# Stick-breaking attention: the second scan of a unit is issued one step later, behind the copy of the first head's transposed weights, and the copies on VectorE are always the first head's

## The chip, the cores and the metric

The kernel runs on one core of one Trainium2 chip. The metric is the device time of one execution in microseconds (us), and less is better. Engines are named as in the profile: PE is TensorE (PEld its weight loads), DVE VectorE, ACT ScalarE, POOL GpSimd, SP the engine that issues most DMAs.

## What is computed

The model has two layers on 2048 tokens of width 1024. The first layer mixes three kinds of attention: stick-breaking (6 heads of 64), differential (6 heads) and attention to a memory. The change touches only stick-breaking attention, which the reference writes, for each block of 128 queries, as

```
z = einsum('bqhd,bkhd->bhqk', qi, k) * scale
log_1mb = where(strict, log_sigmoid(-z), 0.0)
rc = flip(cumsum(flip(log_1mb, -1), -1), -1)
after = rc - log_1mb
w = where(strict, exp(log_sigmoid(z) + after), 0.0)
out = einsum('bhqk,bkhd->bqhd', w, v)
```

So a weight is the sigmoid of its own score times the product of sigmoid(-z) over all later keys: a running product from the last key to the first.

## The kernel before

The program has these stages: projections of layer 1, stick-breaking, differential attention (with part of the output projection mixed in), the join, and layer 2. Each engine works through its own queue in the order of the program; the queues meet at semaphores.

In stick-breaking (L543 to L650) heads go in pairs: p counts three pairs, t four chunks of 512 queries (from the last to the first), qi four blocks of 128 queries in a chunk, and c the chunks of 512 keys, from the diagonal back to the first. A **unit** (p, t, qi, c) is one block of queries against one chunk of keys for both heads of the pair, 120 units in all, 84 of them 512 keys wide and the others, on the diagonal, 384, 256 or 128. A unit passes four functions:

- `scores(u)`: TensorE writes the scores of both heads into a PSUM tile `psz` (2 buffers).
- `weights(u)`: ScalarE takes two sigmoids of it, `s` (of -z) and `wb` (of z), both heads in one instruction each. Then for each head VectorE runs a scan over `s` (a running product, written into `row`; 0 is added from the PSUM tile `pszero`), and GpSimd multiplies `wb` by `row` (L608).
- `turn(u)`: for each head TensorE transposes the 128-wide blocks of `wb` into a PSUM tile `pstp` (2 buffers), and the tile is copied to SBUF as `wT`. `tblocks` (L472) does both. The copy's engine comes from a pattern that is used letter by letter, A for ScalarE and V for VectorE: with "AAV" over the calls the units repeat in threes: both copies on ScalarE; first head on VectorE and second on ScalarE; first on ScalarE and second on VectorE.
- `values(u)`: TensorE multiplies `wT` with the values into `pspv`. Two units' products are issued together, after every second turn.

The loop over units k issues scores(k+3), turn(k), weights(k+3), and every second time the products of units k-2 and k-1. TensorE, VectorE, ScalarE and the DMAs keep exactly this order (they are pinned, and all their rows carry line L57); GpSimd's is left to the scheduler. At the start of a chunk, `begin` issues the DMAs for the next: for the chunk (2, 1) these are also the loads that differential attention and the first output products need (`kc`, `kd`, `qa`, `mp`, and `rx`, which are weights of the output projection). The scheduler also decides which of the two `pstp` buffers a tile gets, and with that which copy it has to wait for.

Of the kernel before, what the change touches and what calls it, by code (L numbers as in the profile page):

```python
# [17 lines left out]
P = 128  # L18
# [21 lines left out]
SB_AHEAD = 3  # L40
# [26 lines left out]
class Net:  # L67
# [475 lines left out]
    def stick_breaking(self):  # L543

        nc = self.nc
        self.nc = PinnedCore(nc, self.tc, ("sync", "tensor", "vector", "scalar"))
        chunks = [(p, t) for p in range(3) for t in range(NT - 1, -1, -1)]
        units = [(p, t, qi, c) for p, t in chunks for qi in range(3, -1, -1) for c in range(t, -1, -1)]  # L550
        kv, qs, sls, prs, zs, ws, wTs, pvs = {0: self.sb_first[:2]}, {(0, NT - 1): self.sb_first[2]}, {}, {}, {}, {}, {}, {}

        def begin(p, t):
            sls[p, t] = self.load_silu(self.silu[p], t)
            k = chunks.index((p, t)) + 1
            if k < len(chunks):
                qs[chunks[k]] = self.load_qstack(self.sbq[chunks[k][0]], chunks[k][1])
            if t == NT - 2 and p < 2:
                kv[p + 1] = self.load_sb(p + 1)
            if p == 2 and t == FT:  # L560
                self.fill = self.filler()
                steps.extend(next(self.fill))
                for f in steps[:4]:
                    f()
                del steps[:4]
                self.dk, self.dq = {}, {}
                self.load_dq(0, 0, 0)
                for c in range(NT):
                    self.load_dk(0, c)

        def bounds(u):
            p, t, qi, c = u
            n = (4 * t + qi + 1) * P
            return n, c * 512, min(n, c * 512 + 512)

        def scores(u):
            p, t, qi, c = u
            n, lo, hi = bounds(u)
            m, diag, s0 = hi - lo, hi == n, int(lo == 0)
            if qi == 3 and c == t:  # L580
                begin(p, t)
            if c == t:
                prs[p, t, qi] = [self.t("row", F32, [P, 2048]) for _ in range(2)]
                for hh in range(2):
                    nc.gpsimd.memset(prs[p, t, qi][hh][:, n - 1:n], 1.0)
            z = self.psum("z", [P, 2, 512])
            for hh in range(2):
                for k in range(2):
                    self.nc.tensor.matmul(z[:, hh, :m], qs[p, t][:, hh, k, qi * P:(qi + 1) * P], kv[p][0][hh][:, lo:hi], start=(k == 0),
                                          stop=(k == 1 and not diag))  # L590
                if diag:
                    self.nc.tensor.matmul(z[:, hh, m - P:m], self.identb, self.mask[:, 2 * P + 1:3 * P + 1], start=False, stop=True)
            zs[u] = z

        def weights(u):
            p, t, qi, c = u
            n, lo, hi = bounds(u)
            m, s0, z = hi - lo, int(lo == 0), zs.pop(u)
            rest = self.t("s", F32, [P, 2, 512])
            self.nc.scalar.activation(rest[:, :, :m], z[:, :, :m], AF.Sigmoid, scale=-0.125)  # L600
            w = ws[u] = self.t("wb", F32, [P, 2, 512])
            self.nc.scalar.activation(w[:, :, :m], z[:, :, :m], AF.Sigmoid, scale=0.125)
            for hh in range(2):
                prr = prs[p, t, qi][hh]
                self.nc.vector.tensor_tensor_scan(
                    prr[:, lo + s0 - 1:hi - 1][:, ::-1], rest[:, hh, s0:m][:, ::-1], zero.to_broadcast([P, m - s0]),
                    prr[:, hi - 1:hi], ALU.mult, ALU.add)
                nc.gpsimd.tensor_mul(w[:, hh, :m], w[:, hh, :m], prr[:, lo:hi])  # L608

        def turn(u):  # L610
            n, lo, hi = bounds(u)
            w = ws.pop(u)
            wTs[u] = [self.tblocks([w[:, hh, j:j + P] for j in range(0, hi - lo, P)], "AAV") for hh in range(2)]

        def values(u):
            p, t, qi, c = u
            n, lo, hi = bounds(u)
            if qi == 3 and c == t:
                pvs[p, t] = self.psum("pv")
            pv, wT, nj = pvs[p, t], wTs.pop(u), (hi - lo) // P  # L620
            for j in range(nj):
                for hh in range(2):
                    self.nc.tensor.matmul(pv[64 * hh:64 * hh + 64, qi * P:(qi + 1) * P], kv[p][1][:, 4 * c + j, 64 * hh:64 * hh + 64],
                                          wT[hh][:, j * P:(j + 1) * P], start=(hi == n and j == 0), stop=(c == 0 and j == nj - 1))
            if qi == 0 and c == 0:
                mt = self.t("c2")
                self.nc.vector.tensor_mul(mt, pvs.pop((p, t)), sls.pop((p, t)))
                self.dma(self.m1[p, :, t * TC:(t + 1) * TC], mt, nc.scalar if p == 2 and t == 0 else None)

        done, steps = 0, []  # L630
        zero = self.psum("zero")[:, :1]
        nc.vector.memset(zero, 0.0)
        for u in units[:SB_AHEAD]:
            scores(u)
            weights(u)
        for k, u in enumerate(units):
            if k + SB_AHEAD < len(units):
                scores(units[k + SB_AHEAD])
            turn(u)
            if k + SB_AHEAD < len(units):  # L640
                weights(units[k + SB_AHEAD])
            if u[0] == 2 and k > len(units) - 11:
                for f in steps[:1]:
                    f()
                del steps[:1]
            while k - done >= SB_GROUP or k == len(units) - 1 and done <= k:
                for v in units[done:done + SB_GROUP]:
                    values(v)
                done += SB_GROUP
        self.nc = nc  # L650
# [872 lines left out]
```

## Time and profile before

| what | value |
|---|---|
| median of 3 runs | 2544.74 us (2543.16 to 2546.1) |
| profiled execution, its own time | 2546.16 us |
| its span, first to last instruction | 2544.4 us |
| granted TensorE clock, mean over the span | 0.984 |
| stick-breaking, first scan to last transpose copy | about 722 to 1076 us |

The span is what the trace covers; the rest of an execution's own time, 1.8 us here, lies around it. All times in rows are counted from the start of the span. Busy shares are means over stages with different limits, so what follows is read from the stick-breaking stage alone.

### The profile page before, as it was taken

Reading aid. Unit: us, or ns where it says so; the run is one execution under the profiler, and the core shown is the slowest. Engines: PE = TensorE matmul, PEld = TensorE weight load, DVE = VectorE, ACT = ScalarE, POOL = GpSimd, SP = SyncE. Lnnn points to the kernel's source line nnn. Section 1 sums busy time; section 2 is a strip of 40 time slices with the busy share of each in tenths; the row PEclk is TensorE's granted clock in tenths of the full one; section 3 lists DMA queues with packets and bytes.
Section 4 is the critical chain, followed back from the end, with each engine's and each line's share of the span. In section 5 each row is a group of like instructions: output and inputs, shape, how many; then the busy total and the mean of one; then the engine's idle time right before and its main releaser. Section 6 shows DMA issues by size and latency. Waiting matters only on the chain. (4 is left out here: it accounts for less than half of the span.)

```text
span 2544.4 us, 42300 instructions
## 1 busy us (share of the span) xinstructions
PE 2392.6 (94%) x15564; PEld 1939.8 (76%) x15564; DVE 1573.6 (62%) x3657; ACT 1254.2 (49%) x2453; POOL 939.3 (37%) x800
## 2 busy tenths in 40 slices
PE   9999999999999999789889888899999999999998
PEld 7778998888877777557667666778788777777887
DVE  5733222431168888699899899684312676777455
ACT  4443222221158777567677677443212777776100
POOL 0401002750057878611111021464612655534333
PEclk9999999999999999899999999999999999999999
DMA  7643222331334431944543341563323655533641
GB/s 280 208 156 131 82 84 79 127 132 56 107 90 111 93 84 34 215 122 109 128 112 94 103 109 46 181 204 109 86 98 112 163 153 154 144 97 101 199 144 64
DMA packets 199247, 311.60 MB, mean 122 GB/s; under 512 B 17920, under 2 KB 97280, under 8 KB 198528
## 3 DMA queue, kind: packets, MB, share of 16 engines
q1 hardware_dynamic: 198464, 307.83, 40.8%
q8 instruction: 124, 2.03, 0.4%
q10 hardware_dynamic: 576, 1.05, 0.1%
q14 instruction: 83, 0.68, 0.1%
HBM read 204.74 MB, written 104.07 MB: 121 GB/s over the span
## 5 line engine op out<-in xcount | busy, mean ns | idle before, releaser
L57 PE MATMUL psmm<-big,w 128*128 128x512 f32 x1680 | 414.9, 395 | 1.3 <-ACT c L325 1.3
L57 PEld LDWEIGHTS psmm<-big,w 128*128 128x128 f32 x1680 | 306.6, 189 | 59.4 <-ACT c L325 1.5
L57 ACT COPY wT<-pstp 128x512 f32<-128x512 f32 (+3 forms) x400 | 203.4, 525 | 188.6 <-PE pstp L57 185.0
L608 POOL TENSOR_TENSOR wb<-wb,row 128x512 f32<-128x512 f32 (+3 forms) x240 | 262.6, 1117 | 72.8 <-DVE row L57 47.5
L57 DVE TENSOR_TENSOR_SCAN row<-s,row,pszero 128x512 f32<-128x512 f32 (+5 forms) x240 | 254.3, 1105 | 51.8 <-ACT s L57 33.4
L254 PE MATMUL psmm<-big,w 128*128 128x512 f32 x1200 | 275.2, 390 | 0.0
L254 PEld LDWEIGHTS psmm<-big,w 128*128 128x128 f32 x1200 | 225.1, 188 | 46.9 <-issue 0.2
L57 PE MATMUL psmm<-big,mp 128*128 128x512 f32 x1056 | 246.6, 394 | 3.4 <-POOL big L1015 3.4
L57 ACT ACTIVATE row<-row,mn 128x2048 f32<-128x2048 f32 (+7 forms) x192 | 229.8, 1202 | 13.9 <-DVE mn L781 10.1
L57 PEld LDWEIGHTS psmm<-big,mp 128*128 128x128 f32 x1056 | 199.7, 190 | 45.3 <-POOL big L1015 3.8
L775 DVE TENSOR_SCALAR_CACHE_REDUCE row<-psz 128x512 f32<-128x512 f32 (+1 forms) x324 | 200.2, 640 | 20.7 <-PE psz L57 19.8
L1234 DVE TENSOR_TENSOR c<-psmm,c 128x512 f32<-128x512 f32 x62 | 42.7, 691 | 240.3 <-ACT c L1233 240.3
L945 POOL TENSOR_TENSOR mp<-mp,mp 128x640 fp32r<-128x640 f32 x32 | 52.0, 1625 | 343.4 <-ACT mp L57 282.7
L57 PE MATMUL pstp<-ident,wb 128*128 128x128 f32 x816 | 118.2, 277 | 35.4 <-DVE wT L57 15.4
L817 DVE SCALAR_TENSOR_TENSOR row<-row,tiny,row 128x128 f32<-128x128 f32 (+7 forms) x144 | 149.4, 1088 | 0.4
L57 PE MATMUL psmm<-wo,mp 128*128 128x512 f32 x480 | 147.7, 420 | 1.4 <-POOL mp L945 0.9
L209 POOL TENSOR_TENSOR w<-w,w 128x1024 fp32r<-128x1024 f32 x20 | 48.8, 2440 | 256.3 <-ACT w L208 107.5
L1233 ACT ACTIVATE c<-psmm 128x512 f32<-128x512 f32 x62 | 36.8, 596 | 212.8 <-PE psmm L254 204.5
L57 PE MATMUL pstp<-ident,row 128*128 128x128 f32 x816 | 130.5, 281 | 6.4 <-ACT wT L57 5.6
L57 PEld LDWEIGHTS pstp<-ident,wb 128*128 128x128 f32 x816 | 92.2, 141 | 56.6 <-POOL wb L608 24.8
L1191 ACT ACTIVATE e<-e,tiny 128x256 f32<-128x256 f32 (+1 forms) x192 | 94.7, 494 | 60.5 <-DVE e L1189 60.1
L57 PEld LDWEIGHTS pstp<-ident,row 128*128 128x128 f32 x816 | 99.6, 143 | 30.8 <-ACT wT L57 13.4
(232 smaller groups left out, 5003.0 us busy)
## 6 DMA issues: line engine op xcount, KB each, us to landing
silu<-c SPq DMA_DIRECT2D x54, 256.0 KB, 2.3
sl<-silu SPq DMA_DIRECT2D x54, 256.0 KB, 3.3
qs<-sbq SPq DMA_DIRECT2D x48, 256.0 KB, 5.3
cs<-rope SPq DMA_DIRECT2D x24, 512.0 KB, 4.6
kc<-k SPq DMA_DIRECT2D x36, 320.0 KB, 5.0
w<-in_we_dram SPq DMA_DIRECT2D x20, 512.0 KB, 3.6
raw<-in_wo_dram SPq DMA_DIRECT2D x20, 512.0 KB, 3.8
rx<-in_x_dram SPq DMA_DIRECT2D x32, 256.0 KB, 2.7
```

What stands on the lines that cost most here:

```text
L57: return self.tc.keep_in_program_order(f(*a, **k))
L209: eng.tensor_sub(lo[:, sl], raw[:, sl], hi[:, sl].bitcast(F32))
L254: self.nc.tensor.matmul(ps, w[a][:, c, :], self.xpart(t, c, b), start=(c == k == 0), stop=(c == 7 and k == 2))
L608: nc.gpsimd.tensor_mul(w[:, hh, :m], w[:, hh, :m], prr[:, lo:hi])
L775: nc.vector.tensor_scalar(e[:, col + lo:col + lo + n0], z[:, :n0], -scale, before, ALU.mult, ALU.min, accum_out=acc)
L817: self.nc.vector.scalar_tensor_tensor(x[:, lo:hi], y[:, lo:hi], cf[hh][:, w:w + 1], x[:, lo:hi], ALU.mult, ALU.add)
L945: self.nc.gpsimd.tensor_sub(ml, m, mh.bitcast(F32))
L1191: nc.scalar.activation(e[:, hh, ns:], e[:, hh, ns:], AF.Exp, bias=nmx[:, hh:hh + 1], scale=-1.0, accum_out=s[:, hh:hh + 1])
L1233: nc.scalar.activation(sg, ps, AF.Sigmoid)
L1234: nc.vector.tensor_mul(sg, ps, sg)
```

## The change

A unit's two scans are now issued apart. `weights(k+3)` still issues both sigmoids and the first head's scan with its product, but the second head's scan and product are put off into a list. The next step's `turn` takes them out after it has issued the first head's transposes and their copy, and before the second head's transposes. So in step k VectorE's queue has: copy of unit k's first head, second scan of unit k+2, first scan of unit k+3. The patterns change too: the first heads' copies go V, V, A, and the second heads' copies are all on ScalarE. As before, two units in three have one copy on VectorE.

```
             w = ws[u] = self.t("wb", F32, [P, 2, 512])
             self.nc.scalar.activation(w[:, :, :m], z[:, :, :m], AF.Sigmoid, scale=0.125)
-            for hh in range(2):
+
+            def scan(hh):
                 prr = prs[p, t, qi][hh]
                 self.nc.vector.tensor_tensor_scan(
                     prr[:, lo + s0 - 1:hi - 1][:, ::-1], rest[:, hh, s0:m][:, ::-1], zero.to_broadcast([P, m - s0]),
                     prr[:, hi - 1:hi], ALU.mult, ALU.add)
                 nc.gpsimd.tensor_mul(w[:, hh, :m], w[:, hh, :m], prr[:, lo:hi])
+            scan(0)
+            second.append(lambda: scan(1))
 
         def turn(u):
             n, lo, hi = bounds(u)
             w = ws.pop(u)
-            wTs[u] = [self.tblocks([w[:, hh, j:j + P] for j in range(0, hi - lo, P)], "AAV") for hh in range(2)]
+            wTs[u] = []
+            for hh in range(2):
+                wTs[u].append(self.tblocks([w[:, hh, j:j + P] for j in range(0, hi - lo, P)], "A" if hh else "VVA"))
+                if second and not hh:
+                    second.pop(0)()
...
         for u in units[:SB_AHEAD]:
             scores(u)
             weights(u)
+            if u != units[SB_AHEAD - 1]:
+                second.pop(0)()
```

The rows below show the program's order at units 58 to 63, in the second pair of heads. A scan stands in them as SCALAR_TENSOR_TENSOR, the numbers are those of the tiles, and a line's two `row` tiles are the first and the second head's.

VectorE before: `s_8076` is unit 61's, `s_8124` unit 62's, `s_8151` unit 63's; `pstp_8062` is the first head of unit 58 and `pstp_8118` the second head of unit 59.

```order
L57 SCALAR_TENSOR_TENSOR row_7978<-s_8049,row_7978,pszero_5912 128x512
L57 SCALAR_TENSOR_TENSOR row_7979<-s_8049,row_7979,pszero_5912 128x512
L57 COPY wT_8067<-pstp_8062 128x512
L57 SCALAR_TENSOR_TENSOR row_7978<-s_8076,row_7978,pszero_5912 128x511
L57 SCALAR_TENSOR_TENSOR row_7979<-s_8076,row_7979,pszero_5912 128x511
L57 COPY wT_8122<-pstp_8118 128x384
L57 SCALAR_TENSOR_TENSOR row_8101<-s_8124,row_8101,pszero_5912 128x256
L57 SCALAR_TENSOR_TENSOR row_8102<-s_8124,row_8102,pszero_5912 128x256
```

VectorE now, from the first scan of unit 60 on (`s_8049`): `pstp_8060` is the first head of unit 58 and `pstp_8135` the first head of unit 60.

```order
L57 SCALAR_TENSOR_TENSOR row_7976<-s_8049,row_7976,pszero_5912 128x512
L57 COPY wT_8065<-pstp_8060 128x512
L57 SCALAR_TENSOR_TENSOR row_7977<-s_8049,row_7977,pszero_5912 128x512
L57 SCALAR_TENSOR_TENSOR row_7976<-s_8076,row_7976,pszero_5912 128x511
L57 SCALAR_TENSOR_TENSOR row_7977<-s_8076,row_7977,pszero_5912 128x511
L57 SCALAR_TENSOR_TENSOR row_8099<-s_8124,row_8099,pszero_5912 128x256
L57 COPY wT_8140<-pstp_8135 128x512
L57 SCALAR_TENSOR_TENSOR row_8100<-s_8124,row_8100,pszero_5912 128x256
```

A copy stood behind both scans of a unit two steps ahead; it now stands behind the first of them alone, and the second scan comes after it. Where the three-unit pattern has no copy on VectorE (unit 59 here) the two scans stand together as before.

ScalarE before, at the turns of units 59 and 60 and the sigmoids of units 62 and 63:

```order
L57 COPY wT_8116<-pstp_8112 128x384
L57 ACTIVATE s_8124<-psz_8105 128x2x256
L57 ACTIVATE wb_8126<-psz_8105 128x2x256
L57 COPY wT_8142<-pstp_8137 128x512
L57 COPY wT_8149<-pstp_8144 128x512
L57 ACTIVATE s_8151<-psz_8132 128x1024
```

ScalarE now, at the same place:

```order
L57 COPY wT_8114<-pstp_8110 128x384
L57 COPY wT_8122<-pstp_8118 128x384
L57 ACTIVATE s_8124<-psz_8103 128x2x256
L57 ACTIVATE wb_8126<-psz_8103 128x2x256
L57 COPY wT_8149<-pstp_8144 128x512
L57 ACTIVATE s_8151<-psz_8130 128x1024
```

Of every three units, one (unit 59) had its sigmoids behind the first head's copy alone. Now the sigmoids of every unit stand behind a copy of a second head's transposes. The number of copies on ScalarE is the same. TensorE's instructions stand in the same order as before through the whole program.

## Rows read from the trace of the kernel before

**Rows 1.** Busy time, share of the span and instructions of each engine, whole span

```profile
PE 2392.6 (94%) x15564; PEld 1939.8 (76%) x15564; DVE 1573.6 (62%) x3657; ACT 1254.2 (49%) x2453; POOL 939.3 (37%) x800
```

**Rows 2.** Busy time in one stretch of stick-breaking: each engine's us (instructions), granted clock, DMA

```profile
core 0: us, PE busy (x) PEld busy (x) DVE busy (x) ACT busy (x) POOL busy (x), PEclk, DMA share, GB/s
740.00:1018.00 278.00, 261.85 (x2510) 213.35 (x2507) 246.76 (x275) 220.48 (x331) 221.57 (x276) 1.00 0.32 75
```

**Rows 3.** Waits in the stretch 740 to 1018: us in total, times, longest us

```profile
ACT wT L57 <- PE pstp L57: 56.8, 63, 2.3
...
DVE row L57 <- ACT s L57: 27.8, 31, 2.2
...
PE pstp L57 <- DVE wT L57: 12.4, 22, 1.5
...
PE pstp L57 <- POOL wb L608: 2.1, 4, 0.8
...
DVE wT L57 <- PE pstp L57: 1.1, 2, 0.7
```

**Rows 4.** Timeline of VectorE, 889 to 899: start us, us, instructions, idle before

```profile
890.26 2.46 DVE L57 TENSOR_TENSOR_SCAN row<-s,row,pszero 128x512 f32<-128x512 f32 x2 [0.71 <-ACT s L57]
892.62 0.67 DVE L57 COPY wT<-pstp 128x512 f32<-128x512 f32 x1
893.21 2.44 DVE L57 TENSOR_TENSOR_SCAN row<-s,row,pszero 128x511 f32<-128x511 f32 x2
895.56 0.54 DVE L57 COPY wT<-pstp 128x384 f32<-128x384 f32 x1
896.01 1.38 DVE L57 TENSOR_TENSOR_SCAN row<-s,row,pszero 128x256 f32<-128x256 f32 x2
898.51 1.28 DVE L57 TENSOR_TENSOR_SCAN row<-s,row,pszero 128x512 f32<-128x512 f32 x1 [1.12 <-ACT s L57]
```

**Rows 5.** Timeline of TensorE, 889 to 899

```profile
893.04 0.92 PE L57 MATMUL pstp<-ident,wb 128*128 128x128 f32 x6
893.71 1.18 PE L57 MATMUL psz<-kd,qs 128*128 128x512 f32 x4
894.73 0.60 PE L57 MATMUL pstp<-ident,wb 128*128 128x128 f32 x4
896.24 0.63 PE L57 MATMUL pstp<-ident,wb 128*128 128x128 f32 x4 [0.92 <-DVE wT L57]
896.80 1.75 PE L57 MATMUL pspv<-wT,kd 128*64 128x128 f32 x28
```

**Rows 6.** Timeline of ScalarE, 889 to 899

```profile
896.96 0.58 ACT L57 COPY wT<-pstp 128x512 f32<-128x512 f32 x1 [1.01 <-PE pstp L57]
897.45 1.03 ACT L57 ACTIVATE s<-psz 128x1024 f32<-128x1024 f32 x1
```

**Rows 7.** Groups of VectorE's instructions, 740 to 1018: xcount | busy us, mean ns | idle before

```profile
L57 DVE TENSOR_TENSOR_SCAN row<-s,row,pszero 128x512 f32<-128x512 f32 x77 | 94.2, 1267 | 18.7 <-ACT s L57 18.4 <-issue 0.2
L57 DVE COPY wT<-pstp 128x512 f32<-128x512 f32 x47 | 31.5, 670 | 0.8 <-PE pstp L57 0.7
```

**Rows 8.** Copies by engine, 740 to 1018: ns min/median/max, first and last start us, forms

```profile
L57 ACT COPY wT<-pstp x132: 265/586/687, 741.7 to 1017.4; 128x512 f32<-128x512 f32 x95, 128x256 f32<-128x256 f32 x14, 128x384 f32<-128x384 f32 x12, 128x128 f32<-128x128 f32 x11
L57 DVE COPY wT<-pstp x67: 264/667/692, 740.8 to 1017.0; 128x512 f32<-128x512 f32 x47, 128x384 f32<-128x384 f32 x7, 128x128 f32<-128x128 f32 x7, 128x256 f32<-128x256 f32 x6
```

**Rows 9.** Timeline of SP's DMA issues, 900 to 1075

```profile
1018.34 3.59 SPq L57 DMA_DIRECT2D qs<-sbq  x4
...
1048.27 8.82 SPq L113 DMA_DIRECT2D kd<-dfk  x8
1057.96 0.35 SPq L57 DMA_DIRECT2D rx<-in_woute_dram  x1
```

**Rows 10.** Waits of SP's DMA queue, 900 to 1080: us in total, times, longest us

```profile
SPq L57 <- PE psz L57: 27.3, 1, 27.3
```

**Rows 11.** Timeline of ScalarE, 1050 to 1135, at the end of stick-breaking

```profile
1067.02 0.62 ACT L57 CAST wo<-rx 128x512 fp32r<-128x512 f32 x1 [15.34 <-DMA rx<-in_woute_dram]
```

**Rows 12.** Timeline of TensorE, 1050 to 1135

```profile
1052.88 1.31 PE L57 MATMUL pspv<-wT,kv 128*64 128x128 f32 x20
1068.27 0.87 PE L57 MATMUL pstp<-ident,wb 128*128 128x128 f32 x3 [14.08 <-ACT wT L57]
```

**Rows 13.** Waits in the whole stage, 718 to 1077

```profile
PE pstp L57 <- DVE wT L57: 15.4, 26, 1.5
```

More of the change, by code (lines that the diff above doesn't have):

```diff
@@ L602, in weights, with scan @@
             self.nc.scalar.activation(w[:, :, :m], z[:, :, :m], AF.Sigmoid, scale=0.125)
-            for hh in range(2):
+            def scan(hh):
                 prr = prs[p, t, qi][hh]
@@ L608, in weights @@
                 nc.gpsimd.tensor_mul(w[:, hh, :m], w[:, hh, :m], prr[:, lo:hi])
+            scan(0)
+            second.append(lambda: scan(1))
         def turn(u):
@@ L612, in turn @@
             w = ws.pop(u)
-            wTs[u] = [self.tblocks([w[:, hh, j:j + P] for j in range(0, hi - lo, P)], "AAV") for hh in range(2)]
+            wTs[u] = []
+            for hh in range(2):
+                wTs[u].append(self.tblocks([w[:, hh, j:j + P] for j in range(0, hi - lo, P)], "A" if hh else "VVA"))
+                if second and not hh:
+                    second.pop(0)()
         def values(u):
@@ L628, in values @@
                 self.dma(self.m1[p, :, t * TC:(t + 1) * TC], mt, nc.scalar if p == 2 and t == 0 else None)
-        done, steps = 0, []
+        done, steps, second = 0, [], []
         zero = self.psum("zero")[:, :1]
@@ L635, in stick_breaking @@
             weights(u)
+            if u != units[SB_AHEAD - 1]:
+                second.pop(0)()
         for k, u in enumerate(units):
```

## Prediction

> **What bounds the kernel now.** I read the page first: TensorE is busy 94% of the span and VectorE 62% [rows 1], but these are means over stages, and the change lives in one. So I read the table of busy times for that stage, from 740, when the pipeline is full, to 1018, where the loads of the next stage begin. There TensorE is busy 261.85 of 278.00 us and VectorE 246.76, ScalarE 220.48, GpSimd 221.57, with the clock at full grant [rows 2]. No engine is full. TensorE has 16.2 us idle, VectorE 31.2.
>
> The list of waits says who holds whom [rows 3]. TensorE's own waits are few: 12.4 us in 22 waits for a VectorE copy out of a `pstp` buffer, 2.1 us in 4 for GpSimd's products. VectorE idles 27.8 us for ScalarE's `s`, and ScalarE 56.8 us for transposes. So it is a ring. The timeline shows one turn of it. The copy of unit 59's second head stands behind both scans of unit 61 and starts at 895.56, when they are through [rows 4]. Its transposes had been done long before: they are among the six at 893.04 [rows 5]. The buffer is free at 896.1, and only then, at 896.24, can TensorE transpose unit 60's second head, after 0.92 us of idling [rows 5]. ScalarE copies that at 896.96 after 1.01 us of idling, takes the next `s` at 897.45 [rows 6], and VectorE's next scan, at 898.51, has waited 1.12 us for it [rows 4]. So one late copy on VectorE costs TensorE, ScalarE and VectorE about 1 us each, one after the other. From the scan at 893.21 to the scan at 898.51 the ring took 5.3 us for two units.
>
> What do the engines need for two full units? Scans follow each other every 1.2 us (two from 893.21 to the next start at 895.56), and a copy of 0.67 has 0.59 to the next start [rows 4, 7]. Two units are four scans and on average 4/3 copies: 4.7 + 0.8 = 5.5 us. The ring is as long as the work, so any unevenness shows as a wait. That is how I read a stage in which nobody is full.
>
> At the stage's end something else binds. TensorE stands still for 14.08 us before 1068.27 [rows 12], because ScalarE waits 15.34 us for a weight load `rx` [rows 11]. That load is issued at 1057.96, behind a train of loads that SP starts at 1018.34 [rows 9], and SP had waited 27.3 us for TensorE's scores before that start, since they free the `qs` buffers [rows 10]. So the train starts when TensorE reaches a certain unit, and ends some 48.7 us later whatever the engines do in between. What is gained before 1018 moves the train and everything behind it; what is gained between 1018 and 1053 only lengthens the 14 us of idling.
>
> **The change, part by part.** No instruction is added or removed; TensorE's order stays, and the two scans, two products and copies of each unit keep their durations.
>
> (a) A VectorE copy moves ahead of one scan, so it starts 1.2 us earlier. The 22 waits of 12.4 us average 0.56, the longest is 1.5 [rows 3]. Moved by 1.2, all but the longest go, and of that one at most 0.3 is left: **-12**. From below the bound is nothing (another wait ends at the same moment), from above TensorE's whole idle time in the stretch, 16.2 [rows 2]. The whole stage has 4 more such waits, 3.0 us [rows 13]; some of them lie behind 1018, where they are covered by the loads, so I count none.
>
> (b) A copy now can be wanted sooner. The first head's tile is often the buffer that the next unit's first transposes need, and where no products stand between, TensorE comes back to it after four transposes and one block of scores: about 0.5 + 1.0 us (894.73 and 896.24 give 0.56 for four transposes up to the products; 893.71 to 894.73 the scores [rows 5]). A copy that starts as its tile is done takes 0.67 [rows 7]; with VectorE up to a scan of 1.2 behind it is done at 1.9, late by up to 0.4. Products stand between at every second step, so about half of the 67 copies [rows 8] are exposed. From 0 to 33 x 0.4 = 13 us. I take 0.06 for each of the 33, **+2**, since VectorE is that far behind only where it has no idle time before a scan, and 31 scans do have it [rows 3].
>
> (c) The second scan comes one copy later, 0.59 us, and so do GpSimd's product and the transposes behind it. TensorE waits for products only 4 times, 2.1 us [rows 3], and the transposes come two units later, some 5.5 us. The cover is this lead of two units: **0**. Without it, 67 x 0.59 = 40 us.
>
> (d) The copies on VectorE are now in front of a scan, so a copy whose transposes aren't done holds a scan. Today the copy waits for them twice, 1.1 us [rows 3], because it stands 1.2 later. If a third of the 67 copies waited half of that, VectorE would lose 22 x 0.6 = 13 us; it has 31.2 idle [rows 2], and the held scan is the one with two units of lead: **0**, at worst 13.
>
> (e) Every unit's sigmoids now follow the second head's copy. In one unit of three (199 copies [rows 8] are about 100 units, so 33 units) they followed the first's, and now come later by four transposes, 0.45 to 0.6 [rows 5]. From 0 to 33 x 0.6 = 20 us on ScalarE's path to VectorE. VectorE has a second scan of the unit before and a copy to do meanwhile, and in the other two units this is already so. I take a twentieth, **+1**.
>
> (f) A few DMA issues and GpSimd instructions change places around the boundary to the next stage: the last stores and loads of `m` before two of `rx`. One issue takes 0.35 us [rows 9]: **0**, within 1 either way.
>
> Sum: -12 + 2 + 1 = -9. The profiled execution took 2546.16, 1.4 above the median of the runs; 2546.16 - 9 = 2537, against the median 2544.74 - 9 = 2535.7. I say **2536**. As a check, the stretch would be 269 us, with TensorE 97% and VectorE 92% busy, which still leaves slack.
>
> **The rivals.**
>
> *VectorE is the bound, and order doesn't help it.* VectorE's work stays 246.76 us, and its idle time stays if ScalarE's `s` comes no sooner: then TensorE's waits for copies turn into waits for products. For it: with 5.5 us of work for two units VectorE has no margin over the ring. Against it: its own idle time in the example comes from its own late copy. Time: no change, 2542 to 2547.
> The Trainium skill bears on this (Perfetto Trace Analysis, Identifying the Most-Contended Engine): it says matmul busy share is no good measure of TensorE and weight-load busy share is to be used, while for VectorE occupancy is fair. By it TensorE stands at 213.35 of 278, 77%, and VectorE at 89% [rows 2] is the engine to relieve, which this change doesn't do; it would give the time of this rival. The rows agree on the order of the two shares, not on its conclusion, since VectorE's idle time begins with a wait that its own copies cause.
>
> *The gain is hidden by the load train.* If the train ended at a fixed time, 2545. Against it: SP's 27.3 us wait for the scores [rows 10] ties its start to TensorE. I put it with the first.
>
> *Slower: the sigmoids behind the second head.* Place: ScalarE at 33 units. Price: up to 0.6 each, 20 us, less the 12 of (a): +8, 2553. It decides against the change from a delay of 0.52 a unit that nothing covers (17 - 12 = +5). For it: 27.8 us of VectorE's idle time end with `s` [rows 3]. Against it: two units in three live with it already, and VectorE's queue holds a scan more at that moment.
>
> *More than I count.* All of TensorE's idle time goes: -16.2 and up to 2 from the stage's opening, 2527.
>
> **How the numbers follow.** Forecast (2531 to 2539.5) 0.51, more than I count 0.11, no change or hidden 0.25, slower 0.13. A difference of 0.2%, 5.1 us, is about what a measurement of this kernel can tell from none. Faster 0.62, same 0.25, slower 0.13. The range, 2527 to 2548, leaves out the slower rival and a tail below; the likeliest case's own range is 2531 to 2539.5.
>
> **What would show it.** (a) right: TensorE's waits for a VectorE copy before 1010 fall from 12.4 to under 4. (b): what is left of them stands before first heads. (d): VectorE's waits for transposes rise from 1.1 to several us, without a longer stage. (e) wrong: VectorE's idle time for `s` rises over 27.8. The stretch from 740 to SP's `qs` issue, now at 1018.34, should end near 1009, with the idle time before the `rx` cast still about 15. If the stage ends sooner and the whole doesn't, the loads hid it; if TensorE's waits go and VectorE's for `s` grow as much, VectorE was the bound.

## The result, and the profile after

| what | before | after |
|---|---|---|
| median of the runs, us | 2544.82 (2543.16 to 2546.1, 4 runs) | 2531.59 (2527.61 to 2532.59, 4 runs) |
| ratio | | 0.9943, 95% interval 0.993 to 0.9956 |
| profiled execution, us | 2546.16 | 2527.61 |

The change made the kernel 13.2 us faster. The forecast was 2536, in a range of 2527 to 2548; the time lies just inside the low end of the likeliest case's own range, 2531 to 2539.5. The profiled execution is the fastest of the four, so its 18.6 us overstate the gain. Of the executions below one, of the kernel with three buffers, took 3348.97 us at a granted clock of 0.651, against 0.973 in the profiled one, and is left out of that kernel's numbers.

TensorE runs the same 15564 matmuls in the same order in both traces, so equal ones can be laid side by side. At the last matmul before stick-breaking the execution after is 1.1 us ahead (718.3 against 719.4), before the change acts. The lead then grows through the stage: 4.0 at 800.6, 8.4 at 868, 11.4 at 933, and 14.7 when SP issues `qs`. So the stage gives 13.6 up to there; the prediction had put that issue near 1009. From there to the end of the program 3.9 more come in small steps, which the median doesn't confirm.

Busy time of each engine from 740 to SP's `qs` issue, now at 1003.66, in the columns of [rows 2]:

```profile
740.00:1003.66 263.66, 257.72 (x2496) 212.50 (x2495) 244.82 (x273) 218.26 (x329) 221.92 (x272) 1.00 0.35 79
```

The stretch took 278.34 us and takes 263.66. TensorE's idle time in it went from 16.2 to 5.9, VectorE's from 31.6 to 18.8, while VectorE's work per unit is the same. (The stretch after starts 1.7 us further on in the program, the lead at 740, so it holds 16 matmuls fewer.) The waits of that stretch, which answer to [rows 3] (us in total, times, longest us), with the weight loads' own:

```profile
ACT wT L57 <- PE pstp L57: 45.1, 53, 2.1
...
DVE row L57 <- ACT s L57: 10.5, 17, 1.6
...
PEld pstp L57 <- POOL wb L609: 6.1, 9, 1.1
...
PE pstp L57 <- DVE wT L57: 3.8, 8, 0.7
DVE wT L57 <- PE pstp L57: 3.5, 8, 0.8
```

VectorE's copies hold TensorE for 3.8 us where it was 12.4, and VectorE idles 10.5 us for ScalarE's `s` where it was 27.8. The row of PEld was not among the rows before the prediction. The kernel before has this one, in the list for the weight loads from 740 to 1018.34:

```profile
PEld pstp L57 <- POOL wb L608: 20.1, 28, 1.2
```

Most waits for GpSimd's products (`wb`) are recorded at the transposes' weight loads: 20.1 us in 28 before, 6.1 in 9 after. The rows of PE showed 4 of them, 2.1 us, and show none now. The two lists can't be added: before, 12.4 of TensorE's 16.2 us of idle time end with VectorE's copies, so most of the 20.1 lies beside matmuls that were still running.

VectorE's timeline after, which answers to [rows 4]:

```profile
881.39 1.28 DVE L57 TENSOR_TENSOR_SCAN row<-s,row,pszero 128x512 f32<-128x512 f32 x1 [0.16 <-ACT s L57]
882.59 0.67 DVE L57 COPY wT<-pstp 128x512 f32<-128x512 f32 x1
883.17 4.25 DVE L57 TENSOR_TENSOR_SCAN row<-s,row,pszero 128x512 f32<-128x512 f32 x4
887.33 0.67 DVE L57 COPY wT<-pstp 128x512 f32<-128x512 f32 x1
887.92 1.91 DVE L57 TENSOR_TENSOR_SCAN row<-s,row,pszero 128x256 f32<-128x256 f32 x2
```

Each copy starts behind one scan and the put-off scan follows it. The x4 is the unit in three whose copies are both on ScalarE.

At the stage's end, SP's issues [rows 9] and ScalarE's cast [rows 11] after:

```profile
1003.66 3.18 SPq L57 DMA_DIRECT2D qs<-sbq  x4
...
1033.03 8.05 SPq L113 DMA_DIRECT2D kd<-dfk  x8
1042.08 0.35 SPq L57 DMA_DIRECT2D rx<-in_woute_dram  x1
```

```profile
1051.28 0.62 ACT L57 CAST wo<-rx 128x512 fp32r<-128x512 f32 x1 [15.66 <-DMA rx<-in_woute_dram]
```

The train of loads starts 14.7 us sooner (before: 1018.34), the `rx` for which ScalarE waits is the first behind it and is issued 15.9 sooner (1057.96), the wait is as long as before, 15.7 against 15.3, and the cast starts 15.7 sooner. Behind a stall of the same length the gain arrives whole.

One row was misread in the prediction. The wait of 27.3 us [rows 10] stands before the `qs` issue at 983.86, not before the one that starts the train. SP's waits in the kernel before, from 985 to 1019, show the right one:

```profile
SPq L57 <- PE pstp L57: 16.6, 1, 16.6
```

It is a wait for TensorE too, so the train's start is tied to TensorE as the prediction said.

### The profile page after: what moved, and what is told of

Read it like the earlier page. It is cut to its first block, busy times and chain, and to the rows that moved or that the text cites. A ratio compares the mean times of both kernels' runs of the same rounds, so it can differ in the third digit from the quotient of the medians.

```text
span 2525.8 us, 42259 instructions
## 1 busy us (share of the span) xinstructions
PE 2384.6 (94%) x15564; PEld 1935.1 (77%) x15564; DVE 1571.6 (62%) x3657; ACT 1253.6 (50%) x2453; POOL 946.3 (37%) x800
## 5 line engine op out<-in xcount | busy, mean ns | idle before, releaser
L57 PE MATMUL pstp<-ident,wb 128*128 128x128 f32 x816 | 112.1, 276 | 23.2 <-ACT wT L57 15.4
```

The costliest lines, as they stand in the source:

```text
L57: return self.tc.keep_in_program_order(f(*a, **k))
```

## Experiments

The **theory**: a VectorE copy that stands behind one scan less comes free sooner, and the ring of transposes, ScalarE's copy, sigmoids and scans gets shorter. The rivals: the gain comes from the patterns alone, or from the split alone; VectorE's work is the bound; the train of loads hides the gain; the place of the sigmoids costs much more than was taken. Ratios are to the kernel before, run on the same chip, with 95% intervals.

**The patterns alone** (kernel before):

```diff
-  ... "AAV") for hh in range(2)]
+  ... "A" if hh else "VVA") for hh in range(2)]
```

> Only the copy patterns of the change (first heads V, V, A, second heads always A); both scans of a unit stay together, so a VectorE copy still stands behind two scans. Theory (the ring through the late copy): TensorE's waits for VectorE copies stay near 12 us before the load train and the time stays within 0.2% of before, 2540 to 2550. Rival (which head's copy is on VectorE is what matters): the gain of the change, 2530 to 2535. A third view (sigmoids behind the second head's copy cost something): slower than before by up to 8, 2545 to 2553.

Measured: 2548.44 (2546.17 to 2550.44), ratio 1.0015 (1.0006 to 1.0023), 3.7 us slower. Its waits from 740 to the `qs` issue at 1021.04:

```profile
ACT wT L57 <- PE pstp L57: 59.9, 69, 2.1
...
DVE row L57 <- ACT s L57: 27.0, 33, 2.2
PEld pstp L57 <- POOL wb L608: 22.6, 30, 1.8
...
PE pstp L57 <- DVE wT L57: 13.2, 24, 1.4
```

The rows are within 3.1 us of those of before. Which head is copied on VectorE brings no gain while the copy stands behind two scans. The 3.7 us also fit the third view in the expectation: here every unit's sigmoids stand behind a second head's copy, as after the change, while no VectorE copy leaves its place behind two scans. That makes this run the nearest to a price for that place, term (e).

**The split alone** (changed kernel, with the old pattern):

```diff
-  ... "A" if hh else "VVA"))
+  ... "AAV"))
```

> Only the split of the scans, with the old copy pattern A, A, V over the calls. One VectorE copy in two (the first heads') moves ahead of a scan; the other (second heads', issued after the put-off scan) stays behind both scans as before. Theory (late copies): between a third and two thirds of the gain, 2535 to 2541, with half of TensorE's waits for VectorE copies left (4 to 9 us). Rival (the split itself, by letting GpSimd start sooner or evening VectorE's queue): the whole gain, 2530 to 2534. Rival (patterns): no gain, 2543 to 2547.

Measured: 2540.82 (2536.97 to 2544.8), ratio 0.9985 (0.9976 to 0.9994), 4.0 us faster. With "AAV" half of VectorE's copies are of second heads, and those come after the put-off scan, so they still stand behind both. Waits from 740 to 1012.72:

```profile
DVE row L57 <- ACT s L57: 17.7, 20, 2.0
PEld pstp L57 <- POOL wb L609: 15.1, 17, 1.7
PE pstp L57 <- DVE wT L57: 12.9, 15, 2.3
```

The waits for copies stay at 12.9, where 4 to 9 were expected; `s` and the products come sooner. Counting transposes and copies off in program order tells whose copies they are: in the kernel before 11 of the 22 waits (3.8 us) end with a first head's copy and 11 (8.6) with a second head's; here all 15 end with a second head's. So no wait is left for the copies that moved ahead of a scan, and those that did not move hold TensorE longer. The longest, unit 42's, with VectorE's queue before it:

```profile
842.68 0.63 PE L57 MATMUL pstp<-ident,wb 128*128 128x128 f32 x4 [2.27 <-DVE wT L57]
```

```profile
840.69 1.26 DVE L57 TENSOR_TENSOR_SCAN row<-s,row,pszero 128x511 f32<-128x511 f32 x1
841.88 0.66 DVE L57 COPY wT<-pstp 128x512 f32<-128x512 f32 x1
```

Alone the parts give +3.7 and -4.0, together -13.2: the effect is one of both.

**The dose, the other way** (kernel before, each VectorE copy held back behind the first scan of unit k+3):

```diff
+        if held is not None and pattern[self.turns.get(pattern, 0) % len(pattern)] == "V":
+            self.turns[pattern] += 1
+            held.append(lambda: self.nc.vector.tensor_copy(o[:, :n * P], ps[:, :n * P]))
+        else:
             self.evac(o[:, :n * P], ps[:, :n * P], pattern)
...
                 nc.gpsimd.tensor_mul(w[:, hh, :m], w[:, hh, :m], prr[:, lo:hi])
+                if held:
+                    held.pop(0)()
```

> The kernel before with each VectorE copy moved one scan the other way: behind both scans of the unit two ahead and the first scan of the unit three ahead. Theory (the ring grows by a scan of 1.2 us for every copy): TensorE's waits for VectorE copies grow from 12 us to 40 or more, and the time by 25 to 80, 2570 to 2625. Rival (VectorE's work is the bound, order alone moves waits about): within 5 of before, 2540 to 2550.

Measured: 2586.98 (2580.02 to 2588.84), ratio 1.0161 (1.0147 to 1.0175), 42 us slower, with VectorE's work unchanged (247.62 us to the `qs` issue at 1054.64). Waits of that stretch:

```profile
ACT wT L57 <- PE pstp L57: 92.2, 75, 3.5
...
DVE row L57 <- ACT s L57: 54.4, 51, 3.1
...
PE pstp L57 <- ACT wT L57: 24.7, 21, 1.7
PEld pstp L57 <- POOL wb L612: 23.7, 21, 1.9
...
PE pstp L57 <- DVE wT L57: 15.6, 20, 1.8
```

The total is that of a ring, but TensorE's waits are not where I looked for them: VectorE's copies hold it for 15.6, ScalarE's for 24.7, the weight loads wait 23.7 for products, and VectorE idles 54.4 for `s`. In these rows a late copy spreads round the ring and is booked where the next engine happens to wait. The step isn't one of a scan's duration alone: the copy now also stands behind a scan that needs the next unit's `s`, so 42 us is not the price of 1.2 us a copy.

**The train: the new order before it, and behind it** (changed kernel; the units of the third pair from chunk (2, 1) on are those whose gain comes after the train starts). The first has the old order for those units, the second only for all others:

```diff
-            second.append(lambda: scan(1))
+            if not (u[0], -u[1]) >= (2, -FT):      # the second run: without "not", and without the pops before the loop
+                second.append(lambda: scan(1))
+            else:
+                scan(1)
...
-  ... "A" if hh else "VVA"))
+  ... ("A" if hh else "VVA") if not (u[0], -u[1]) >= (2, -FT) else "AAV"))
```

> The changed order and patterns for all units up to chunk (2, 2), the old ones for the chunks (2, 1) and (2, 0), whose units run while the load train does. Theory (the train hides what is gained behind its start): as the changed kernel, 2529 to 2534, with ScalarE's wait for the rx load shorter by about what the last units lose. Rival (part of the gain comes from the last units or the boundary): 2534 to 2540.

> The reverse: the old order and patterns up to chunk (2, 2), the changed ones only in the chunks (2, 1) and (2, 0). Theory (hidden behind the train): as before, 2542 to 2547, with a wait for the rx load of 15 us or more. Rival (the end of the stage gives 2 us or more of the gain, by the new order of stores and loads at the boundary): 2538 to 2542.

Measured: 2532.43 (2530.13 to 2534.44), ratio 0.9952 (0.994 to 0.9964); and 2546.13 (2542.7 to 2548.94), ratio 1.0006 (0.9997 to 1.0014). The units ahead of the train carry the whole gain, the later ones nothing that shows.

**The copies of the second head on VectorE** (changed kernel, with heads exchanged in the copies, and the put-off scan behind the second head's copy):

```diff
-  ... "A" if hh else "VVA"))
-                if second and not hh:
+  ... "VVA" if hh else "A"))
+                if second and hh:
```

> The split of the scans, but VectorE's copies are the second heads' (V, V, A) and ScalarE copies every first head; the put-off scan comes after the second head's copy, so a copy again stands behind one scan only, and two sigmoids in three follow the first head's copy. Theory that the place of the copy in VectorE's queue is all: as the changed kernel, 2528 to 2534. Rival that the sigmoids behind the second head's copy cost 5 us or more in the changed kernel: faster than it, 2520 to 2527. Rival that a copy of the second head holds VectorE's put-off scan for transposes that come 0.45 us later: slower than the changed kernel, 2534 to 2542.

Measured: 2526.61 (2525.69 to 2527.9), ratio 0.9931 (0.9919 to 0.9944), 18.2 us faster than before and 5.0 below the changed kernel's median, with overlapping intervals. Busy times and waits from 740 to the `qs` issue at 997.92:

```profile
740.00:997.92 257.92, 255.15 (x2489) 212.03 (x2488) 242.09 (x272) 216.66 (x327) 220.77 (x272) 1.00 0.35 81
```

```profile
DVE wT L57 <- PE pstp L57: 7.8, 10, 1.5
...
DVE row L57 <- ACT s L57: 5.6, 8, 1.5
...
PEld pstp L57 <- POOL wb L609: 2.3, 5, 0.9
...
PE pstp L57 <- DVE wT L57: 0.9, 2, 0.7
```

TensorE is busy 99% of the stretch. VectorE waits more for transposes than in the kernels above, 7.8, and idles least for `s`, 5.6: copies that wait for their transposes did not keep this version from being the fastest so far.

**Is it the head, or the place of the sigmoids?** (changed kernel; the second head goes first in the turn, so it is copied on VectorE and yet the sigmoids again stand behind the copy of the tile transposed last.)

```diff
-            wTs[u] = []
-            for hh in range(2):
-                wTs[u].append(... "A" if hh else "VVA"))
-                if second and not hh:
+            wTs[u] = [None, None]
+            for hh in (1, 0):
+                wTs[u][hh] = ... "VVA" if hh else "A")
+                if second and hh:
```

> The changed kernel with the roles of the heads in the turn exchanged: the second head's transposes come first, their copies go V, V, A, the put-off scan follows, and then the first head's transposes, whose copies are all on ScalarE. So second heads are copied on VectorE, behind one scan, as in the version with second-head copies, but every unit's sigmoids stand behind the copy of the head that is transposed last, as in the changed kernel. Theory (the sigmoids behind the last copy are what the changed kernel loses against the version with second-head copies, about 5 us): as the changed kernel, 2529 to 2534, with VectorE's idle time for s between 740 and the qs issue at about 10 us. Rival (it matters which head's copy goes to VectorE, or which head's scan is put off): as the version with second-head copies, 2524 to 2528, with that idle time at about 6.

Measured: 2534.29 (2527.52 to 2535.22), ratio 0.9951 (0.9939 to 0.9964): as the changed kernel. The interval still overlaps with that of the version above, but the stage parts them: the `qs` issue comes at 1005.72, where it came at 1003.66 after the change and at 997.92 in the version above. Waits from 740 to 1005.72:

```profile
DVE row L57 <- ACT s L57: 12.1, 24, 1.5
PEld pstp L57 <- POOL wb L609: 8.4, 16, 0.9
...
DVE wT L57 <- PE pstp L57: 3.6, 9, 0.8
...
PE pstp L57 <- DVE wT L57: 2.5, 7, 0.6
```

VectorE idles 12.1 us for `s`, as after the change and twice what it does above. So which head VectorE copies doesn't decide it; the order within the turn does. That order holds three things the times don't part: the sigmoids, when a copied buffer is wanted again (2.5 us of waits for copies here, 0.9 above), and that the head whose scan is put off is here transposed first, so that its product is wanted sooner (weight loads wait 8.4 for products, above 2.3).

**A third `pstp` buffer.** PSUM has room for one if the scan's zero leaves it, so there are two kernels, a control with the zero in SBUF, and the control with three buffers:

```diff
-        zero = self.psum("zero")[:, :1]
-        nc.vector.memset(zero, 0.0)
+        zero = self.zero
...
-  {"z": 2, "tp": 2, "pv": 1, "zero": 1}
+  {"z": 2, "tp": 2, "pv": 1}               # then "tp": 3
```

> The kernel before, with the scan's added zero read from SBUF in place of PSUM, which frees a PSUM bank and is the base for the next run. If the scans then hold GpSimd's products up (two SBUF inputs beside GpSimd's): products of 1.28 us or scans of 1.26 us get longer and the time grows by 20 or more, over 2565. If not: within 5 of before.

> As the one before, with the freed bank as a third buffer for transposes, in the old order of scans and copies. Theory (a late copy hurts only because its buffer is wanted): against the run with two buffers TensorE's waits for VectorE copies fall from about 12 to under 3 us and the time by 8 to 16. Rival (VectorE or ScalarE is the bound, or the waits move to the product with the values): within 4 of the run with two buffers.

Measured: the control 2655.2 (2653.97 to 2656.75), ratio 1.0436 (1.0422 to 1.0449); with three buffers 2653.43 (2650.81 to 2654.78), ratio 1.0428 (1.0414 to 1.0441). The control alone is 110.6 us slower. Busy times from 740 to its `qs` issue, and the groups of GpSimd's products and VectorE's scans (xcount | busy us, mean ns | idle before):

```profile
740.00:1125.89 385.89, 303.41 (x2594) 244.83 (x2594) 368.52 (x281) 226.76 (x336) 353.11 (x283) 0.91 0.24 54
```

```profile
L608 POOL TENSOR_TENSOR wb<-wb,row 128x512 f32<-128x512 f32 x146 | 289.9, 2013 | 29.1 <-DVE row L57 27.8 <-PE pstp L57 1.2
L57 DVE TENSOR_TENSOR_SCAN row<-s,row,zero 128x512 f32<-128x512 f32 x80 | 133.5, 1711 | 9.6 <-ACT s L57 9.6
```

A wide scan takes 1711 ns where it took 1267 [rows 7], and a wide product 2013 where the same list for before has 1282. VectorE is busy 368.52 of 385.89 us, so here it is the bound; the granted clock, 0.99 to 1.00 in the stretches above, is 0.91 on average in this one, with TensorE busy 303.41 us. The third buffer takes the waits for copies from 77.8 us (second group) to 20.6, and what is left turns into waits for products; from 740 to 1119.37:

```profile
PE pstp L57 <- POOL wb L608: 35.0, 38, 1.5
PE pstp L57 <- DVE wT L57: 20.6, 9, 3.3
```

For the question of buffers the pair is inconclusive: the waits for copies fall by 57 us, and the time by 1.8, under a bound that keeps it.

**The length of the train** (before, changed, and with second-head copies; the first loads for differential attention, `qa`, `kc` and `kd`, are issued one chunk sooner):

```diff
+            if p == 2 and t == FT + 1:
+                self.dk, self.dq = {}, {}
+                self.load_dq(0, 0, 0)
+                for c in range(NT):
+                    self.load_dk(0, c)
...
-                self.dk, self.dq = {}, {}
-                self.load_dq(0, 0, 0)
-                for c in range(NT):
-                    self.load_dk(0, c)
```

> The kernel before, with the loads for differential attention (qa, kc and kd, some 24 issues and 22 us of SP's time) moved from the start of chunk (2,1) to the start of the chunk before it, so that the train of loads ahead of rx is shorter. Theory (the 14 us of idling at the end of stick-breaking is the length of that train): ScalarE's wait for rx is gone or under 3 us, and the time is 2529 to 2534. Rival (rx is held by something else than the issues ahead of it, or another load takes its place): 2541 to 2547.

> The changed kernel with the same loads moved to the start of the chunk before. Theory (the train hides what the change gains behind its start, 2 to 3 us, and costs 14): 2514 to 2519, that is 14 to 16 below the kernel before with the loads moved. Rival (the stall at the end has another cause): 2527 to 2533.

> The version with second-head copies on VectorE, with the same loads moved to the start of the chunk before. Theory (the stall at the end goes, and the first heads' copies leave about 5 us that the second heads' don't): 2508 to 2513, 4 to 7 below the changed kernel with the loads moved. Rival on the heads (no difference between them): 2514 to 2519, like the changed kernel with the loads moved. Rival on the stall: 2522 to 2528.

With `qa` the moved loads are 32 issues (8, 12 and 12), 28.7 us of SP's time in the kernel before; the 24 and 22 of the first expectation fit `kc` and `kd` alone.

Measured on one chip, beside 2545.63 for the kernel before: 2534.95 (2529.12 to 2535.16), ratio 0.9954 (0.9941 to 0.9966); 2516.98 (2512.58 to 2518.17), ratio 0.9888 (0.9874 to 0.9901); 2510.8 (2507.28 to 2511.9), ratio 0.9864 (0.9849 to 0.9879). SP's issues in the second, where the loads now go ahead of the `qs` issue that ends the stretch, and TensorE's waits for ScalarE's copies from 960 to 1100, first in the changed kernel, then with the loads moved:

```profile
974.74 5.24 SPq L57 DMA_DIRECT2D qa<-dfq  x8
...
1008.11 3.88 SPq L57 DMA_DIRECT2D qs<-sbq  x4
...
1027.33 0.33 SPq L57 DMA_DIRECT2D rx<-in_woute_dram  x1
...
1032.06 0.33 SPq L57 DMA_DIRECT2D rx<-in_woute_dram  x1
```

```profile
PE pstp L57 <- ACT wT L57: 15.4, 2, 14.7
```

```profile
PE pstp L57 <- ACT wT L57: 0.9, 2, 0.7
```

The stall of 14.7 us is 0.7, and the second list has no wait for `rx`. The kernel before gains 10.7 this way, a little less than expected (2529 to 2534), the changed one 14.6, the third 15.8. With the train out of the way the change is worth 18.0 (2534.95 to 2516.98), and the copies on the second head 6.2 more; the runs of the last two don't overlap. The last is the best version, 34.8 us below the kernel before.

## Why the prediction held

**The mechanism** is shown by the copies that moved and those that didn't: with half of them ahead of a scan, every wait left is for the other half. The dose goes the same way: VectorE's copies one scan later 42 us slower, one scan sooner 13.2 faster, with VectorE's work the same in all three. **The size** was too small: 9 forecast, 13.2 measured (13.6 in the stage). That 2531.59 lies so near 2536 is in part luck: the row that the sum was built on gave less than was taken from it, (e) cost more than was taken, and (c), put at nothing, made up for both and more.

**(a), -12, was mis-sized.** Its own row moved by 8.6 (12.4 to 3.8; under 4 was forecast), where (a) and (b) together took 10 from it. The rest was never in that row: the weight loads' waits for products fell by 14.0, which I had not listed, and what a weight load waits shows only in part as idle time of PE. Over the same 2508 matmuls, from the one at 740 before to SP's `qs` issue, TensorE's idle time fell by 10.2 (16.1 to 5.9) and its busy time by 2.8 (262.3 to 259.5), 13.0 in all. (The other 1.7 of the 4.5 by which the busy time of the two stretches differs is the program that the stretch after doesn't hold.) The busy time that went is the transposes': their 682 records last 275 and 274 ns each, but cover 97.5 us before and 92.4 after. So they stand closer together, and I read that as waits during which an earlier matmul was still counted as busy. That is also why the upper bound, TensorE's idle 16.2, is none: the version with second-head copies gains 18.1 in the stage up to there (20.4 at its `qs` issue, less 2.3 at the stage's start).

**(b), +2,** was right in kind and near in size. What is left is 3.8 us in 8 waits, one of 0.74:

```profile
904.68 1.04 PE L57 MATMUL pstp<-ident,wb 128*128 128x128 f32 x8
905.49 1.17 PE L57 MATMUL psz<-kd,qs 128*128 128x512 f32 x4
907.39 1.06 PE L57 MATMUL pstp<-ident,wb 128*128 128x128 f32 x8 [0.74 <-DVE wT L57]
908.39 1.97 PE L57 MATMUL pspv<-wT,kd 128*64 128x128 f32 x32
```

These are transposes, scores, and again transposes with no products between, and the wait is in front of a first head, as in 7 of the 8.

**(c), 0,** was wrong in sign: products did not become late; the waits for them fell, and that is the part of the gain that no term had: 2.1 us of TensorE's idle time and, as I read it, the 2.8 of busy time. Its reason, 4 waits of 2.1 us, rested on the wrong engine's row, and the lead of two units was less than it seemed: 28 weight loads were waiting. **(d), 0,** was right: VectorE's waits for transposes rose from 1.1 to 3.5, and to 7.8 in a version that is faster. **(e), +1,** was too small, though its test (over 27.8 us for `s`) did not fire: with second-head copies two units in three have their sigmoids behind the tile that is transposed first, which is worth 5.0 to 7.7 for some 66 units, so the 33 units of (e) cost perhaps 2.5 to 4. That is an estimate, and the copies' and products' waits are part of it; the patterns alone, which move these sigmoids and no scan, cost 3.7. **(f), 0:** right within what can be told. It was not run by itself.

**The rivals.** *VectorE is the bound* fell: its work stayed, and its idle time shrank by 12.8. What spoke for it was partly a misreading: the ring's 5.3 us in the example are for one wide unit and one of 256 keys, and were set against 5.5 us of work for two wide ones; VectorE's own work in them was 4.2, with 1.1 idle [rows 4]. By the Trainium skill's rule (Perfetto Trace Analysis, Identifying the Most-Contended Engine) VectorE at 89% was the engine to optimize first. The traces don't speak against that: its share rose to 93% after the change and 94% with second-head copies, against 82% of weight loads (212.03 of 257.92). What fell is the step from there to no gain: its idle time could go with no work of its own removed. *Hidden by the train* fell for units ahead of it and holds for those behind. *Slower by the sigmoids* had the right place and a price several times too large, 20 us against 2.5 to 4. *More than I count* was the nearest to the truth that the forecast did not take: it ends at 2527, the forecast at 2536, and 2531.59 lies between.

What stays open: how the 5.0 to 7.7 us of the order within the turn divide between sigmoids, copies and products; why the products' waits fell by as much as they did; and the small steps, up or down by 2 to 4 us, that the profiles show in differential attention.

## What to carry to other kernels

In a ring of engines the place of a short copy in its queue can be worth more than its duration: put it in front of the long instruction that nobody is waiting for yet, and put what feeds the ring in front of the copy that isn't urgent. When waits are counted, read the weight loads' list with the matmuls', and expect a late instruction to be booked on another engine than its own. And look at what stands behind the stage: here loads issued one chunk sooner were worth about as much as the change.

## What the hardware showed that I had not expected

A scan that reads its zero from SBUF rather than PSUM, and GpSimd's product beside it, lengthen each other: 1267 to 1711 ns and 1282 to 2013 ns. It is the overlap and not the place of the zero by itself: in the same trace the five wide scans with no product beside them take 1269 to 1287 ns, and the one wide product with no scan beside it 1276. The Trainium skill (SBUF — State Buffer, Who interferes with whom) says that a VectorE instruction with two SBUF inputs contends with a GpSimd instruction that reads SBUF, and the trace agrees. The Trainium skill also says, on the same page (SBUF: two separate sides), that whichever starts first has the shared ports for its whole instruction and the other is fully blocked. Full exclusion for whole instructions doesn't fit: the stretch's 144 wide scans and 146 wide products at their undisturbed 1267 and 1282 ns, with the narrow ones (32.5 and 41.3 us in the list of after), would need some 443 us one after the other, an estimate, and the stretch is 386.
